# A decoder layer with two attentions: outputs stored as halves and summed in the finish, transposes six steps behind in half 0

## The chip, the cores and the metric

The kernel runs on one core of one Trainium2 chip. The metric is the device time of one execution in microseconds. The kernel before took 2151.33 us, the median of three runs (2150.57 to 2156.12).

## The reference

One decoder layer with two attentions side by side, on 2048 tokens plus 16 learned meta tokens in front, width 1024, float32. Everything comes out of one input projection of 6400 columns.

```python
xn = rms_norm(h, norm_gain[l])
proj = xn @ w_in[l]
sb_q, sb_k, sb_v, sw_q, sw_k, sw_v, sb_z, sw_z, g_sb, g_sw = jnp.split(proj, offsets, axis=-1)
o_sb = stick_breaking_attention(sb_q, sb_k, sb_v, valid)      # 8 heads of 64, all earlier keys
o_sw = sliding_window_sink_attention(q, k, sw_v, sinks, valid) # 16 query heads, 2 key heads, window 128
y_sb = (o_sb * jax.nn.silu(sb_z)) @ w_branch_sb[l]
y_sw = (o_sw * jax.nn.silu(sw_z)) @ w_branch_swa[l]
merged = jax.nn.sigmoid(g_sb) * y_sb + jax.nn.sigmoid(g_sw) * y_sw
h = h + merged @ w_out[l]
return rms_norm(h, final_norm_gain)[:, BLOCK:]
```

The first attention weighs keys by running products of sigmoids (a cumulative sum of logs in the reference), the second is a softmax over the block and the one before it, with a sink. What matters for this change is the line after each of them: the output o of an attention is multiplied by a gate and goes into a branch projection.

## The kernel before, in words

**Precision and tiling.** Most matmul operands are split into a high and a low part of type float32r, and a product is three matmuls (high times high, high times low, low times high). The sequence is processed backwards in four groups of 512 tokens. Groups 2 and 3 are half 0, groups 0 and 1 half 1.

**Stages.** For each half: projections with banded (sliding-window) attention woven in, then gate columns with stick-breaking attention woven in, then more gate columns. Half 0 ends its gates in a "fast" stage with seven products for eight. After both halves comes the finish: for half 0 and then half 1, the branch projections, the merge, the output projection, and the final norm.

**Order.** TensorE's instructions stand in the order of the program, which a function `weave` mixes from a main stream (projections) and a side stream (an attention) by estimated costs. The other engines and the DMA queue are ordered by the framework's planner, by its own estimate of time; each then works strictly in that order. All DMAs are issued by one queue, SP's (`DMA`, line 58).

**Banded attention** (`window`, `values`). For one block of 128 queries and four heads, matmuls accumulate 128 rows in the only PSUM bank `ps_o`: rows 0 to 63 come from the high part of v, rows 64 to 127 from the low part, and the output is their sum. ACT copies the low 64 rows to SBUF (line 757), and two DVE additions (line 761) put the sum into a tile `os`, of which there is one. After four blocks `os` is stored to DRAM as `ow`, in two DMAs.

**Stick-breaking attention** (`stick`). A step is one block of 128 queries against up to 512 keys. `row`: two matmuls into `ps_z` (line 861), a sigmoid on ACT (line 865), and a running product by DVE (`tensor_tensor_scan`, lines 873 and 875). `turn`, LT = 5 steps later: up to four transposes by TensorE into one of two banks `ps_t` (line 886), which ACT and DVE then evict as a high and a low part (`evac_split`, lines 114 and 115). `values`, two steps after that: matmuls into `ps_o` (line 912). At the end of a head and group ACT copies `ps_o` (line 917), a DMA brings its low 64 rows to partitions 0 to 63, POOL adds the two (line 919), and a DMA stores the sum as `od`. In half 0 a head has 12 steps, in all 96; in half 1 it has 28. DVE applies the causal mask in half 0, POOL in half 1.

**Gated tiles** (`gated`). For the branch projections each output tile of 128 x 512 is loaded with its gate (`ow` with `zw`, `od` with `zs`), multiplied by DVE (line 199), cast to the high part by ACT (line 201), and the low part is the difference by DVE (line 202). There are 48 such tiles: 16 of `ow` for half 0, made beside the last gates of half 1 with staging buffers `tmp` (nine of them, shared with the gates); 16 of `ow` for half 1, made while half 0's output projection runs, eight for each group, with staging buffers `a` (AB = 6, shared with other small tiles); and 16 of `od`, eight in each half's finish, with staging buffers `a`.

**Finish** (`finish`). Per half the banded branch comes first: projections `d` = 0, 1, 2 for the first group, the same three for the second group, then `d` = 3 to 7 for both groups. One projection is 24 matmuls (lines 225 to 227) and is multiplied by its gate on DVE (line 253). The `od` tiles are emitted when `d` = 4 begins. Then come the stick-breaking branch, the merge, and the output projection (lines 282 to 284).

Of the kernel before, what the change touches and what calls it, by code (L numbers as in the profile page):

```python
# [7 lines left out]
F32 = mybir.dt.float32  # L8
# [3 lines left out]
ALU = mybir.AluOpType  # L12
# [4 lines left out]
P = 128  # L17
# [4 lines left out]
GT = 512  # L22
RW = GT + NM
NB = SEQ // P
EPS = 1e-6
LT = 5
XS = 4
QB = 4
MID = 3
# [18 lines left out]
def tile_kernel(ctx, tc, x, xt, meta, metat, gain, w_in, w_sb, w_sw, w_out, sinks, fgain,  # L48
# [8 lines left out]
    def DMA(dst, src):  # L57
        nc.sync.dma_start(*(t.bitcast(F32) if t.dtype == F32R else t for t in (dst, src)))
# [28 lines left out]
    def dram(name, shape, dt=F32):  # L87
        return dp.tile(shape, dt, tag=name, name=name)
# [5 lines left out]
    zw = [[dram(f"zw{p}_{g}", [P, GT]) for g in range(4)] for p in range(8)]  # L94
    gs = [[dram(f"gs{p}_{g}", [P, GT]) for g in range(4)] for p in range(8)]
    gw = [[dram(f"gw{p}_{g}", [P, GT]) for g in range(4)] for p in range(8)]
    od = [[dram(f"od{p}_{g}", [P, GT]) for g in range(4)] for p in range(4)]
    ow = [[dram(f"ow{p}_{g}", [P, GT]) for g in range(4)] for p in range(8)]
    ksv = dram("ksv", [P, 4, P], F32R)
    msd = [dram(f"msd{p}", [NM, P]) for p in range(2)]  # L100
    vsv = dram("vsv", [P, 2 * P], F32R)
# [91 lines left out]

    def gated(src, zz, k, g, ring, stg):

        a, b = stg(), stg()
        DMA(a, src[k][g])
        DMA(b, zz[k][g])
        V.tensor_tensor(a, a, b, op=ALU.mult)
        h, l = ring(), ring()  # L200
        A.copy(h, a)
        V.tensor_tensor(l, a, f32(h), op=ALU.subtract)
        return h, l

    def finish(ringl, osw, first):
# [23 lines left out]
        for half, groups in enumerate(halves):  # L229
# [10 lines left out]
            ws_of = {}  # L240
            order = [(d, g) for ds in ([0, 1, 2], *([d] for d in range(3, 8))) for g in groups for d in ds]
            for d, g in order:
                if d == 4 and g == groups[0]:
                    osb = {(k, g): gated(od, zs, k, g, ringr, lambda: small("a", AB)) for g in groups for k in range(4)}
                if d not in ws_of:
                    ws_of[d] = first if half == d == 0 else weights(d * P, w_sw)
                ws = ws_of[d]
                acc = bank()
                project(acc, ws, [osw[k, g] for k in range(8)])
                gt = small("gt", 3)  # L250
                DMA(gt, gw[d][g])
                part[d, g] = ringr(F32)
                V.tensor_tensor(part[d, g], acc, gt, op=ALU.mult)
# [82 lines left out]
    def tmp(dt=F32, rows=P):  # L336
        return tp.tile([rows, GT], dt, tag="tmp", name="tmp", bufs=9)
# [259 lines left out]
    def window(half, groups, sp):  # L597
# [145 lines left out]
        def values(s, g, i, st):  # L743
            kv = s // 2
            blk = 4 * (g - groups[0]) + i
            if i == 0:
                os_[0] = sp.tile([P, 2, GT], F32, tag="os", name="os", bufs=1)
            o = ps("o")
            ph, pl, pm = st["p"]
            oc = o.rearrange("p (a q) -> p a q", a=4)  # L750
            for n in range(2):
                c = slice(HB * n, HB * n + HB)
                v = vv[:, blk + n, kv, :]
                for j, (lv, rp) in enumerate(((v, ph), (v, pl), (dv[kv, blk][:, n, :], pm))):
                    T.matmul(oc[:, :, c], lhsT=lv, rhs=rp[:, :, c], start=j == 0, stop=j == 2)  # L755
            t = tmp(rows=64)
            A.copy(t, o[64:128])
            ov = o[0:64].rearrange("p (b a q) -> p b a q", b=2, a=2)
            tv = t.rearrange("p (b a q) -> p b a q", b=2, a=2)
            for a in range(2):  # L760
                V.tensor_tensor(os_[0][64 * a:64 * a + 64, :, i * P:(i + 1) * P],
                                ov[:, :, a, :], tv[:, :, a, :], op=ALU.add)
            if i == 3:
                for pr in range(2):
                    DMA(ow[2 * s + pr][g], os_[0][:, pr, :])

        os_ = [None]
        ending = []
# [24 lines left out]
    def stick(groups, bp, sums_of={}):  # L793
        kt, vc = {}, {}
        rows_of = {}
        for g in groups:
            w = wm[g % 2]
            G.memset(f32(w), 1.0)
            G.affine_select(out=w, in_=f32(w), pattern=[[-1, 4], [0, P]], compare_op=ALU.is_equal, fill=0.0,
                            base=-64 - 4 * g, channel_multiplier=1)  # L800
# [101 lines left out]
        def values():  # L902

            h, g, v, wh, wl, first, last = av_todo.pop(0)
            st = state[h, g]
            if first:
                st["o"] = ps("o")
            o = st["o"]
            n = wh.shape[1]
            for r in (wh, wl):  # L910
                if r is not None:
                    T.matmul(o[:, :n], lhsT=v, rhs=r, start=first and r is wh, stop=last)  # L912
            if last:
                p, a = divmod(h, 2)
                t = tmp(rows=64)
                u = tmp()
                A.copy(u, o)  # L917
                DMA(t, u[64:128])
                G.tensor_tensor(t, u[0:64], t, op=ALU.add)  # L919
                DMA(od[p][g][64 * a:64 * a + 64], t)  # L920
            return 0.22 if wl is None else 0.43

        steps = [(h, g, n, j) for h in range(8) for g in reversed(groups) for n in range(4 - g) for j in range(4)]
        n = len(steps)
        turned = []
        for s in range(n + LT + 3):
            if s < n:
                row(*steps[s])
                yield 0.45 if s >= LT else 1.31
            t = s - LT  # L930
            if 0 <= t < n:
                turn(*steps[t])
                turned.append(s)
                yield 0.43
                if sum(steps[t][1:3]) == steps[t][3] == 3:
                    turn_meta(*steps[t][:2])
                    turned.append(s)
                    yield 0.43
            while av_todo and turned[0] < s - 1:
                del turned[0]  # L940
                yield values()
# [296 lines left out]
    for half, groups in enumerate(halves):  # L1238
# [57 lines left out]
        with tc.tile_pool(name=f"sb{half}", bufs=1, side="left") as bp:  # L1296
            hsplit[0], vsplit[0] = True, False
            next_sums = {g: sums() for g in halves[1]} if half == 0 else {}
            side = stick(groups, bp, next_sums)
            drain(tiles_by_tile(gts[few:few + 1], groups))  # L1300
            rest = 28 - FAST - PLAIN if half == 0 else 23
            cost_sb = 8 * sum(4 * (4 - g) for g in groups) * 1.31 + 16 * 0.75 + LT * 0.86
            ratio = cost_sb / ((rest - few - 1) * 10.4)
            weave(tiles_by_tile(gts[few + 1:rest], groups), side, ratio)
            if half == 0:
                hsplit[0] = vsplit[0] = True
                plain = [mk() for mk in gts[rest:rest + 2]]
            drain(side)
            if half == 0:
                t, u = (bp.tile([P, GT], F32, tag="wh", name="sum", bufs=3)[:, :8] for _ in range(2))  # L1310
                for n, ssq in enumerate(next_sums.values()):
                    V.tensor_tensor(t[:, 4 * n:4 * n + 4], ssq[:, 0], ssq[:, 1], op=ALU.add)
                rs = tp.tile([P, 8], F32, tag="rs8", name="rs", bufs=1)
                rsqrt(rs, t, tp, t=u)
                rs0, rs1 = rs[:, :4], rs[:, 4:]
# [90 lines left out]
```

## Time and profile before

| | |
|---|---|
| median of three runs | 2151.33 us |
| the profiled execution, its own time | 2154.71 us |
| its span, first to last instruction | 2153.0 us |
| TensorE matmuls, busy | 2118.0 us (98%) |
| VectorE (DVE), busy | 1460.8 us (68%) |
| ScalarE (ACT), busy | 1074.4 us (50%) |
| GpSimd (POOL), busy | 353.2 us (16%) |
| DMA, mean | 180 GB/s |
| mean granted TensorE clock | 0.998 |

How to read it: TensorE is busy nearly all the time, and what is left is idle time spread over the stages. "PE" rows are matmuls, "PEld" rows are weight loads, which run beside them. A row such as "PE ps_t L886 <- DVE wtl L115: 5.8, 11, 1.1" says that matmuls of line 886 waited 5.8 us in total, 11 times, at most 1.1 us, and that a DVE instruction of line 115 ended the wait. In a row of a timeline, the bracket at the end gives the idle time of the engine before it and what ended it. Times of single rows are microseconds from the start of the span.

### The profile page before, as it was taken

The page shows a single profiled execution, that of the slowest core. Times are in us where ns is not written, and L with a number is a line of the kernel's source. Part 1 is how long each engine was busy: PE and PEld are TensorE (multiplying, and loading weights), DVE is VectorE, ACT ScalarE, POOL GpSimd, SP SyncE. Part 2 cuts the span into 40 slices and gives each one's busy share as a digit, 9 for nine tenths or more (in the row PEclk, how much of TensorE's full clock was granted, in tenths as well). Part 3 has the DMA queues.
Part 4 walks back from the last instruction along what each step waited for, and adds up shares of the span by engine and source line. Part 5 has one row for each costly group of instructions (what it writes and reads, how often), then busy time and mean ns, then how long its engine had stood idle before and what let it go on. Part 6 is the DMA issues. An engine that isn't in the chain of part 4 may idle for free.

```text
span 2153.0 us, 30793 instructions
## 1 busy us (share of the span) xinstructions
PE 2118.0 (98%) x10658; PEld 1752.7 (81%) x10658; DVE 1460.8 (68%) x2319; ACT 1074.4 (50%) x2461; POOL 353.2 (16%) x526
## 2 busy tenths in 40 slices
PE   8999999999999999999999999999999999999998
PEld 6788888777778888888888888888888888787886
DVE  7788876877787563777747888878774436453453
ACT  6577775555554334777744555555553213221121
POOL 2234453121110000233310000000100121000000
PEclk9999999999999999999999999999999999999999
DMA  9755454766547674444345333343424976467422
GB/s 331 277 190 194 174 192 165 254 196 193 168 139 252 225 238 158 153 159 162 134 163 173 123 128 118 118 126 96 122 86 157 358 255 219 163 219 272 149 97 88
DMA packets 167740, 386.74 MB, mean 180 GB/s; under 512 B 24192, under 2 KB 28032, under 8 KB 167584
## 3 DMA queue, kind: packets, MB, share of 16 engines
q1 hardware_dynamic: 167584, 384.78, 52.8%
q8 instruction: 84, 1.38, 0.3%
q14 instruction: 72, 0.59, 0.1%
HBM read 237.35 MB, written 140.98 MB: 176 GB/s over the span
## 4 chain that ended last, share of the span: by engine, by line
PE 80%; DVE 7%; ACT 5%; DMA 4%; issue 2%; POOL 1%; SPq 1%; ACTq 0%; POOLq 0%; DVEq 0%
PE ps_g L406 10%; PE ps_g L407 10%; PE ps_g L408 10%; PE ps_o L912 6%; PE ps_z L861 5%; PE ps_t L886 5%; PE ps_z L699 2%; PE ps_o L755 2%; PE ps_g L226 1%; DMA xq<-in_x 1%; PE ps_g L227 1%; PE ps_g L225 1%; PE ps_z L226 1%; PE ps_z L227 1%; PE ps_z L225 1%
## 5 line engine op out<-in xcount | busy, mean ns | idle before, releaser
L406 PE MATMUL ps_g<-xh,wh 128*128 128x512 f32 x1296 | 532.8, 411 | 8.8 <-ACT xh L1090 6.9
L408 PE MATMUL ps_g<-xh,wl 128*128 128x512 f32 x1296 | 509.5, 393 | 0.0
L407 PE MATMUL ps_g<-xl,wh 128*128 128x512 f32 x1296 | 509.2, 393 | 0.0
L875 DVE TENSOR_TENSOR_SCAN row<-row 128x512 f32<-128x512 f32 (+4 forms) x256 | 308.4, 1205 | 84.2 <-POOL row L870 36.6
L408 PEld LDWEIGHTS ps_g<-xh,wl 128*128 128x128 f32 x1296 | 243.8, 188 | 54.5 <-DVE wl L111 0.2
L406 PEld LDWEIGHTS ps_g<-xh,wh 128*128 128x128 f32 x1296 | 245.0, 189 | 48.3 <-ACT xh L1090 6.9
L407 PEld LDWEIGHTS ps_g<-xl,wh 128*128 128x128 f32 x1296 | 245.0, 189 | 38.0 <-DVE xl L1091 1.3
L865 ACT ACTIVATE row<-ps_z 128x512 f32<-128x512 f32 (+1 forms) x320 | 172.2, 538 | 194.2 <-PE ps_z L861 163.1
L114 ACT ACTIVATE wth<-ps_t 128x512 fp32r<-128x512 f32 (+1 forms) x320 | 170.5, 533 | 70.7 <-PE ps_t L886 68.4
L115 DVE SCALAR_TENSOR_TENSOR wtl<-ps_t,wth 128x512 fp32r<-128x512 f32 (+1 forms) x320 | 188.1, 588 | 20.2 <-ACT wth L114 19.7
L861 PE MATMUL ps_z<-kt,q 128*128 128x512 f32 (+3 forms) x640 | 185.8, 370 | 0.2 <-DMA q<-qd 0.2
L886 PE MATMUL ps_t<-ident,row 128*128 128x128 f32 x1088 | 172.4, 274 | 5.9 <-DVE wtl L115 5.8
L886 PEld LDWEIGHTS ps_t<-ident,row 128*128 128x128 f32 x1088 | 134.6, 140 | 43.5 <-DVE wtl L115 10.9
L861 PEld LDWEIGHTS ps_z<-kt,q 128*128 128x128 f32 x640 | 117.8, 188 | 24.3 <-DMA q<-qd 0.6
L912 PE MATMUL ps_o<-wth,vc 128*128 128x512 f32 (+1 forms) x320 | 130.1, 407 | 0.6 <-ACT tmp L917 0.6
L912 PE MATMUL ps_o<-wtl,vc 128*128 128x512 f32 (+1 forms) x320 | 116.7, 365 | 0.0
L707 ACT ACTIVATE sc<-sc,nm 128x129 f32<-128x129 f32 x256 | 100.0, 393 | 31.4 <-DVE nm L705 30.2
L919 POOL TENSOR_TENSOR tmp<-tmp 64x512 f32<-64x512 f32 x32 | 45.5, 1422 | 341.9 <-DMA tmp<-tmp 181.2
L111 POOL TENSOR_TENSOR wl<-raw,wh 128x1024 fp32r<-128x1024 f32 (+1 forms) x28 | 61.4, 2191 | 194.0 <-ACT wh L108 176.9
L108 ACT CAST wh<-raw 128x1024 fp32r<-128x1024 f32 (+1 forms) x44 | 42.7, 971 | 99.6 <-PE ps_g L226 29.7
L873 DVE TENSOR_TENSOR_SCAN row<-row,mask 128x512 f32<-128x512 f32 (+2 forms) x64 | 72.2, 1134 | 29.3 <-ACT row L865 21.1
L561 ACT ACTIVATE tmp<-ps_g 128x512 f32<-128x512 f32 x84 | 50.2, 597 | 59.7 <-PE ps_g L408 53.3
(434 smaller groups left out, 4130.3 us busy)
## 6 DMA issues: line engine op xcount, KB each, us to landing
wh<-h_in_w_in SPq DMA_DIRECT2D x66, 512.0 KB, 3.4
wl<-l_in_w_in SPq DMA_DIRECT2D x66, 512.0 KB, 5.0
raw<-in_w_in SPq DMA_DIRECT2D x50, 512.0 KB, 5.3
h_in_w_in<-wh SPq DMA_DIRECT2D x50, 512.0 KB, 2.7
l_in_w_in<-wl SPq DMA_DIRECT2D x50, 512.0 KB, 3.8
q<-qd SPq DMA_DIRECT2D x128, 128.0 KB, 3.2
vc<-vd SPq DMA_DIRECT2D x48, 256.0 KB, 2.8
kd<-tmp SPq DMA_DIRECT2D x32, 256.0 KB, 3.8
```

The source lines that it names most:

```text
L114: A.activation(h, acc, AF.Copy, scale=scale)
L115: V.scalar_tensor_tensor(l, acc, scale, f32(h), op0=ALU.mult, op1=ALU.subtract)
L406: T.matmul(acc, lhsT=wh[:, k, :], rhs=xh[g][:, k, :], start=k == 0, stop=False)
L407: T.matmul(acc, lhsT=wh[:, k, :], rhs=xl[g][:, k, :], start=False, stop=False)
L408: T.matmul(acc, lhsT=wl[:, k, :], rhs=xh[g][:, k, :], start=False, stop=k == KT - 1)
L707: A.activation(sc[:, hh, :], sc[:, hh, :], AF.Exp, bias=nm[:, hh:hh + 1], accum_out=den[:, hh:hh + 1])
L861: T.matmul(z[:, :w], lhsT=lq, rhs=kt[h][:, k0:k0 + w], start=t == 0, stop=t == 1)
L865: A.activation(r[:, :w], z[:, :w], AF.Sigmoid, scale=-1.0)
L873: V.tensor_tensor_scan(r[:, :w], r[:, :w], mask[:, :w], 1.0, op0=ALU.mult, op1=ALU.max)
L875: V.tensor_tensor_scan(r[:, :w], r[:, :w], r[:, :w], last[j] if n else 1.0, op0=ALU.mult, op1=ALU.min)
L886: T.transpose(tr[:, j * P:(j + 1) * P], rows_of[h, g, n - (j > i), j][:, k0:k0 + P], ident)
L912: T.matmul(o[:, :n], lhsT=v, rhs=r, start=first and r is wh, stop=last)
```

## The change

Four edits that belong together:

- The banded attention copies the whole bank of 128 rows with one ACT copy; the DVE additions are gone. The tile `os` now holds two blocks, and after every second block four DMAs of 128 KB store the high and low halves to `ow`, which is twice as large.
- The stick-breaking attention stores the two halves of its output to `od`, also doubled, straight from ACT's copy; the DMA between partitions and POOL's addition are gone.
- `gated` loads both halves and adds them on DVE before it multiplies by the gate: one more staging buffer, one more DMA of 256 KB and one more DVE addition for each of the 48 tiles. The `od` tiles in the finish are emitted when `d` = 3 begins.
- LT, the lag from `row` to `turn`, is six steps in half 0 and stays five in half 1.

```diff
-LT = 5
+LT = (6, 5)
...
-    od = [[dram(f"od{p}_{g}", [P, GT]) for g in range(4)] for p in range(4)]
-    ow = [[dram(f"ow{p}_{g}", [P, GT]) for g in range(4)] for p in range(8)]
+    od = [[dram(f"od{p}_{g}", [2, P, GT]) for g in range(4)] for p in range(4)]
+    ow = [[dram(f"ow{p}_{g}", [2, P, GT]) for g in range(4)] for p in range(8)]
...
     def gated(src, zz, k, g, ring, stg):
 
-        a, b = stg(), stg()
-        DMA(a, src[k][g])
+        a, b, c = stg(), stg(), stg()
+        DMA(a, src[k][g][0])
+        DMA(c, src[k][g][1])
         DMA(b, zz[k][g])
+        V.tensor_tensor(a, a, c, op=ALU.add)
         V.tensor_tensor(a, a, b, op=ALU.mult)
...
-                if d == 4 and g == groups[0]:
+                if d == 3 and g == groups[0]:
                     osb = {(k, g): gated(od, zs, k, g, ringr, lambda: small("a", AB)) for g in groups for k in range(4)}
...
-            if i == 0:
-                os_[0] = sp.tile([P, 2, GT], F32, tag="os", name="os", bufs=1)
+            if i % 2 == 0:
+                os_[0] = sp.tile([P, 4, 2 * P], F32, tag="os", name="os", bufs=1)
...
-            t = tmp(rows=64)
-            A.copy(t, o[64:128])
-            ov = o[0:64].rearrange("p (b a q) -> p b a q", b=2, a=2)
-            tv = t.rearrange("p (b a q) -> p b a q", b=2, a=2)
-            for a in range(2):
-                V.tensor_tensor(os_[0][64 * a:64 * a + 64, :, i * P:(i + 1) * P],
-                                ov[:, :, a, :], tv[:, :, a, :], op=ALU.add)
-            if i == 3:
+            A.copy(os_[0][:, :, i % 2 * P:(i % 2 + 1) * P], oc)
+            if i % 2:
                 for pr in range(2):
-                    DMA(ow[2 * s + pr][g], os_[0][:, pr, :])
+                    for n in range(2):
+                        DMA(ow[2 * s + pr][g][n][:, (i - 1) * P:(i + 1) * P].rearrange("(a d) t -> d a t", a=2),
+                            os_[0][64 * n:64 * n + 64, 2 * pr:2 * pr + 2, :])
...
+        lt = LT[groups[0] == 0]
...
-                t = tmp(rows=64)
                 u = tmp()
                 A.copy(u, o)
-                DMA(t, u[64:128])
-                G.tensor_tensor(t, u[0:64], t, op=ALU.add)
-                DMA(od[p][g][64 * a:64 * a + 64], t)
+                for n in range(2):
+                    DMA(od[p][g][n][64 * a:64 * a + 64], u[64 * n:64 * n + 64])
...
-        for s in range(n + LT + 3):
+        for s in range(n + lt + 3):
             if s < n:
                 row(*steps[s])
-                yield 0.45 if s >= LT else 1.31
-            t = s - LT
+                yield 0.45 if s >= lt else 1.31
+            t = s - lt
...
-            cost_sb = 8 * sum(4 * (4 - g) for g in groups) * 1.31 + 16 * 0.75 + LT * 0.86
+            cost_sb = 8 * sum(4 * (4 - g) for g in groups) * 1.31 + 16 * 0.75 + LT[half] * 0.86
```

## The prediction

> **What bounds the kernel now.** I read the page first, then a table of stages, then what TensorE waited for. The page gives the frame:
>
> ```profile
> span 2153.0 us, 30793 instructions
> PE 2118.0 (98%) x10658; PEld 1752.7 (81%) x10658; DVE 1460.8 (68%) x2319; ACT 1074.4 (50%) x2461; POOL 353.2 (16%) x526
> ```
>
> TensorE (PE) is the bound, and the change gives it no matmul and takes none away. So its time can move only in the 35 us in which PE sits idle, and in new idle time. The table of stages shows where that is; its columns are length, then busy time (and count) of PE, PEld, DVE, ACT and POOL, the granted clock, the DMA share and GB/s:
>
> ```profile
> 75.00:375.00 300.00, 294.42 (x1655) 249.78 (x1654) 234.32 (x461) 207.68 (x594) 124.96 (x203) 1.00 0.53 187
> 375.00:613.00 238.00, 229.90 (x1259) 189.44 (x1258) 185.67 (x245) 134.33 (x303) 44.91 (x27) 1.00 0.62 194
> 860.00:1125.00 265.00, 261.44 (x1427) 224.06 (x1426) 189.46 (x388) 188.32 (x535) 86.76 (x170) 1.00 0.45 154
> 1125.00:1641.00 516.00, 515.95 (x2780) 430.61 (x2779) 408.16 (x483) 275.47 (x535) 40.30 (x79) 1.00 0.38 119
> 1641.00:1697.00 56.00, 56.00 (x249) 46.36 (x248) 21.66 (x31) 17.94 (x29) 6.07 (x3) 1.00 0.86 305
> 1921.00:2011.00 90.00, 89.78 (x384) 71.80 (x384) 33.63 (x56) 11.06 (x20) 0.00 (x0) 1.00 0.71 248
> ```
>
> The rows are, in order: the banded attention of half 0 (idle 5.6 us), the stick-breaking attention of half 0 (idle 8.1), the banded attention of half 1 (3.6), the stick-breaking attention of half 1 (0.05), the last gates with the first gated tiles (0), and the start of half 1's finish (0.22). There is something to win in the first three, nothing in the fourth, and something to lose in the last two. The list of waits names the releasers:
>
> ```profile
> PE ps_t L886 <- DVE wtl L115: 5.8, 11, 1.1
> PE ps_o L755 <- DVE os L761: 2.5, 3, 1.6
> PE ps_z L699 <- DVE sc L703: 1.0, 4, 0.4
> PE ps_g L226 <- DVE ringl L202: 0.2, 1, 0.2
> ```
>
> All four wait for DVE. The first three are in the attentions, where the change relieves DVE. The fourth is in the finish, where the change loads it.
>
> **Banded attention (values).** Today each block has one ACT copy of 64 rows and two DVE additions that read and then free the one bank ps_o. Now one ACT copy of 128 rows frees it.
>
> ```profile
> L761 DVE TENSOR_TENSOR os<-ps_o,tmp x128: 386/417/419, 136.0 to 1119.0; 64x256 f32<-64x256 f32 x128
> L757 ACT COPY tmp<-ps_o x64: 564/584/590, 134.6 to 1117.9; 64x512 f32<-64x512 f32 x64
> L865 ACT ACTIVATE row<-ps_z 128x512 f32<-128x512 f32 (+1 forms) x320 | 172.2, 538 | 194.2 <-PE ps_z L861 163.1
> ```
>
> DVE loses 128 x 0.417 = 53 us. ACT's copy keeps its 512 columns; a 128-row read of PSUM with 512 columns takes 0.54 us (L865), as much as L757's 0.58, so ACT pays nothing. The three waits on os go: -2.5. The waits on sc (1.0) lose half, since they too wait for DVE: -0.5, bounds 0 and -1. New is a wait of the ACT copy for the stores of the single os tile, now every second block, with four stores in place of two every fourth:
>
> ```profile
> 191.25 0.79 SPq L58 DMA_DIRECT2D ow<-os  x2
> 221.05 0.80 SPq L58 DMA_DIRECT2D ow<-os  x2
> ow<-os SPq DMA_DIRECT2D x32, 256.0 KB, 2.2
> ```
>
> Four blocks take 221.05 - 191.25 = 29.8 us, one 7.5. Four stores issue in 1.6 us and land 2.2 later, 3.8 after the copy, so 3.7 us are left and I take nothing. If SP's queue is held (96 more issues stand ahead of weight loads), ACT waits, and behind it the exponentials and PSUM copies on which PE waits: up to +4, about one microsecond in a quarter of the 16 pairs of a half.
>
> **Stick-breaking attention (row sums and lag).** Gone are 32 SBUF-to-SBUF copies and 32 POOL additions; od's one store becomes two that wait for ACT alone, so the number of DMAs stays. POOL's time itself is free, but not what it does to DVE:
>
> ```profile
> L875 DVE TENSOR_TENSOR_SCAN row<-row 128x512 f32<-128x512 f32 (+4 forms) x256 | 308.4, 1205 | 84.2 <-POOL row L870 36.6
> 510.49 1.27 POOL L919 TENSOR_TENSOR tmp<-tmp 64x512 f32<-64x512 f32 x1 [15.37 <-ACT row L865]
> 511.73 2.38 POOL L111 TENSOR_TENSOR wl<-raw,wh 128x1024 fp32r<-128x1024 f32 x1
> 510.58 4.64 DVE L875 TENSOR_TENSOR_SCAN row<-row 128x528 f32<-128x528 f32 x1 [0.40 <-ACT row L867]
> 516.05 0.55 PE L886 MATMUL ps_t<-ident,row 128*128 128x128 f32 x3 [1.10 <-DVE wtl L115]
> 518.43 0.44 PE L886 MATMUL ps_t<-ident,row 128*128 128x128 f32 x2 [0.50 <-DVE wtl L115]
> ```
>
> A scan that takes 1.2 us on average took 4.64: longer by 3.4, nearly what the two POOL operations ran (1.27 + 2.38). The eviction L115 stood behind it, and PE then waited 1.10 and 0.50 us for a bank. Without L919 the scan keeps only L111's share, some 1.2 us earlier, which covers most of that. From half 0's 5.8 us I take -2.5: this event's 1.6 and 0.9 of the other 4.2. Bounds 0 and -5.8. In half 1 the same contention exists, but PE idles 0.05 us: nothing. SP's queue no longer waits for L919 ahead of the q and xq loads; I count that in the 2.5.
>
> The lag of six in half 0 I price at zero. It gives the scans one more step before their transposes, but PE's waits here are for the evictions of the two ps_t banks (L115), and these come as soon after their transposes as before. It shifts which evictions meet which scans, which can go either way; the bound is one step, 238 us over 104 steps = 2.3 us, to both sides. The ratio of the weave changes by 0.86 in 142, which only shifts gate columns.
>
> **Finish: 48 gated tiles, each with one more load of 256 KB and one more DVE addition.** The tight place is the start of half 1's finish, where eight tiles of group 1 are made while PE runs three projections of group 0:
>
> ```profile
> 1925.92 0.69 DVE L199 TENSOR_TENSOR a<-a 128x512 f32<-128x512 f32 x1
> 1933.28 0.68 DVE L199 TENSOR_TENSOR a<-a 128x512 f32<-128x512 f32 x1
> 1934.70 0.69 DVE L202 TENSOR_TENSOR ringl<-a,ringl 128x512 fp32r<-128x512 f32 x1 [0.74 <-ACT ringl L201]
> 1935.31 0.68 DVE L199 TENSOR_TENSOR a<-a 128x512 f32<-128x512 f32 x1
> a<-od SPq DMA_DIRECT2D x16, 256.0 KB, 5.5
> a<-ow SPq DMA_DIRECT2D x16, 256.0 KB, 3.8
> a<-zw SPq DMA_DIRECT2D x16, 256.0 KB, 4.0
> 1921.28 0.39 PE L225 MATMUL ps_g<-ringl,wh 128*128 128x512 f32 x1
> 1938.07 0.40 PE L225 MATMUL ps_g<-ringl,wh 128*128 128x512 f32 x1
> 1943.02 0.50 PE L225 MATMUL ps_g<-ringl,wh 128*128 128x512 f32 x1
> 1943.75 0.50 PE L226 MATMUL ps_g<-ringl,wh 128*128 128x512 f32 x1 [0.22 <-DVE ringl L202]
> ```
>
> Today one tile costs DVE 0.68 (product), 0.74 (waiting for ACT's cast) and 0.69 (difference), a period of 2.03 us; six buffers "a" hold three tiles in flight. The eighth tile arrives 0.5 us late: the matmul of 1943.75 could have followed at 1943.25. With three buffers a tile only two are in flight. A buffer pair then turns in load 4.0 + issue 0.32 + DVE 0.69 + 0.69 + 0.74 + 0.69 = 7.1 us for two tiles, 3.6 each. The first tile ends at 1925.9 + 2.8 = 1928.7, the second at 1931.5, the eighth at 1931.5 + 3 x 7.1 = 1952.8. PE wants it at 1943.25, so it stands 9.5 us, 9.0 more than now. The lower bound is a DVE that puts the next addition into the 0.74 us gap with all loads in time: 8 x 2.1 + three evictions L253 of 0.68 = 18.9, done at 1944.8, +1.1. The upper takes the landing of a<-od, 5.5: a turn of 8.6, done at 1957.3, +13.6. I take 9, as the loads of today's rows already come into a DMA share of 0.71 over that stage.
>
> Idle PE also costs clock:
>
> ```profile
> 634.00:637.00 3.00, 3.00 (x15) 2.45 (x15) 2.88 (x5) 0.02 (x1) 0.00 (x0) 1.00 0.29 70
> 637.00:641.00 4.00, 2.33 (x9) 1.30 (x8) 3.11 (x5) 4.00 (x7) 0.00 (x0) 0.95 0.61 242
> 641.00:644.00 3.00, 3.00 (x9) 2.32 (x8) 3.00 (x7) 2.62 (x5) 0.00 (x0) 0.50 0.95 265
> ```
>
> After 1.7 idle us in four, the granted clock was 0.50 for the next three, where 9 matmuls ran in place of 15. Waits of 9.5 us within 12 should bring one or two such stretches of 3 us at half speed: +2, bounds 0 and 3.4. The Trainium skill ("TensorE: Matmul & The Clock Gate", Part 1) has the clock fall after at least one idle window of about 3.4 us. By that rule waits cut up by the arrival of single tiles would cost no clock (rival 4); the rows above show a fall after 1.7 us of idling, so the trace does not agree, and it decides.
>
> In half 0's finish 16 such tiles run through nine "tmp" buffers beside the gates: 16 x 256 KB = 4.2 MB more, at 305 GB/s / 0.86 = 355 GB/s another 11.8 us of transfers.
>
> ```profile
> L199 DVE TENSOR_TENSOR tmp<-tmp x16: 684/692/2056, 1659.4 to 1695.8; 128x512 f32<-128x512 f32 x16
> ```
>
> The last is ready at 1695.8 + 2.1 = 1697.9. PE starts this finish at 1697 and, as in half 1, comes to the second group 16.8 us later (1938.07 - 1921.28), at 1713.8. The cover is 15.9 us, 4.1 more than needed. If weight loads stand behind these in SP's queue and get the whole delay, 11.8 - 4.1 = 7.7. I take +2. The eight od tiles, emitted one projection earlier, have 24 loads instead of 16 on SP; they are due only at 2011 and I give them nothing, with one turn (3.6) as upper bound.
>
> **Sum.** -2.5 - 0.5 - 2.5 + 9 + 2 + 2 = +7.5 us. The profiled execution took 2154.71, which makes 2162.2; it lies 3.4 above the median, and against the median of 2151.33 the forecast is 2159.
>
> **Rivals.** (1) Faster: SP and DVE overlap the new additions in the cast's gap, and gated tiles come every 2.1 us, as the lower bound has it. It decides from a period below about 2.4 us in half 1: then 1.1 replaces 9 and 2, half 0 costs nothing, and -5.5 + 1.1 = -4.4 remains; with all of the 5.8 us of bank waits gone in place of 2.5 it is -7.7, and -10 if the lag also gives its 2.3. Its middle is -7.7, 2144, within 2141 to 2147. For it speaks DVE's share in that stage (33.6 of 90 us), against it the six buffers. (2) The two sides cancel: half 1 costs half as much (a turn of 5 to 6 us), 4.5 + 1, total 0, 2150 to 2157; the DMAs' medians hold both fast and slow landings. (3) Half 0's finish stalls too: +7.7 in place of 2, 2165, and up to 2170 with the upper bound in half 1. For it speaks the DMA share of 0.86, against it the 15.9 us of cover. (4) The clock holds through the chopped waits: 2 less, 2157; against it stands the row with 0.50. (5) The lag doesn't do what its name says: that is in the forecast, at zero; if it did, the forecast would read 2157.
>
> **How the numbers follow.** A measurement here tells differences over 0.3%, 6.5 us, so "same" is 2144.9 to 2157.8. Chances: forecast 0.33 (2154 to 2164; 0.26 of it above 2157.8), rival 1 0.24 (0.19 of it faster), rival 2 0.20 (same), rival 3 0.18 (slower), rival 4 0.05 (same). Slower: 0.26 + 0.18 = 0.44. Faster: 0.19. Same: 0.07 + 0.05 + 0.20 + 0.05 = 0.37. The range 2144 to 2168 leaves out the faster half of rival 1 and the top of rival 3; the forecast's own is 2154 to 2164.
>
> **What would show it.** In the list of waits, PE ps_g L226 <- DVE ringl L202 should grow from 0.2 to about 9 us near 1940, with a period of the group-1 tiles near 3.6 us and a row of clock 0.50 behind it; PE ps_o L755 <- DVE os should be gone; PE ps_t L886 should fall from 5.8 to about 3; scans over 2 us beside POOL should be rarer. A period near 2 us there, or PE waits on "a" loads elsewhere, makes the forecast wrong.

## The result, and the profile after

The changed kernel takes **2172.05 us** (median of 6 runs, 2169.81 to 2174.27), the kernel before 2154.68 us beside it (6 runs, 2150.57 to 2157.32): a ratio of **1.0082**, 95% interval 1.007 to 1.0094. The forecast was 2159 in a range of 2144 to 2168: slower was right, the amount was not. The profiled execution took 2170.74.

The page after, first lines:

```profile
span 2168.9 us, 30858 instructions
PE 2124.4 (98%) x10658; PEld 1757.3 (81%) x10658; DVE 1438.9 (66%) x2239; ACT 1066.7 (49%) x2461; POOL 303.2 (14%) x494
```

The same matmuls, 22 us less of DVE and 50 us less of POOL, and a span longer by 15.9 us. The table of stages of the changed kernel shows where (columns as in the prediction):

```profile
75.00:375.00 300.00, 294.97 (x1661) 250.66 (x1661) 217.26 (x403) 202.27 (x593) 126.44 (x202) 1.00 0.63 205
375.00:613.00 238.00, 232.96 (x1272) 194.13 (x1272) 178.14 (x250) 139.58 (x309) 19.66 (x12) 0.99 0.60 192
860.00:1125.00 265.00, 262.62 (x1428) 225.33 (x1427) 160.25 (x313) 178.94 (x524) 82.25 (x169) 1.00 0.54 172
1641.00:1697.00 56.00, 47.91 (x199) 38.46 (x197) 28.73 (x39) 14.94 (x23) 6.27 (x3) 0.94 0.96 350
1921.00:2011.00 90.00, 84.97 (x338) 65.47 (x337) 45.18 (x79) 12.18 (x24) 0.00 (x0) 0.92 0.80 281
```

The attentions (first three rows) idle less than before: 5.0, 5.0 and 2.4 us against 5.6, 8.1 and 3.6. The fourth row, 1641 to 1697, full before (249 matmuls), now idles 8.1 us and has 199 matmuls at a clock of 0.94; the fifth, 1921 to 2011, idles 5.0 us at 0.92. The waits of PE, over the whole span, by releaser:

```profile
PE ps_g L408 <- ACT xh L1087: 6.9, 1, 6.9
PE ps_g L408 <- ACT tmp L563: 6.0, 2, 4.6
PE ps_g L227 <- ACT tmp L563: 5.2, 1, 5.2
PE ps_z L860 <- ACT row L864: 3.2, 2, 2.7
PE ps_g L227 <- ACT ringl L203: 2.9, 3, 1.5
PE ps_g L228 <- DVE ringl L204: 2.0, 3, 0.9
PE ps_t L885 <- DVE wtl L115: 1.6, 3, 1.1
```

Line numbers have moved: the sum in `gated` is L200, its product L201, the cast L203, the difference L204; the projections are L227 to 229, and L563 is the sigmoid in `gate`, which copies a gate column out of PSUM. The first row stands in the kernel before too, with the same 6.9 us. The wait for `os` is not in the list any more, and the wait for L115 fell from 5.8 to 1.6; 3.2 us of waits for L864, a sigmoid of the stick-breaking attention on ACT, are new beside it. The waits for L203 and L204 (4.9) are the forecast one, in half 1. The second and third rows, 11.2 us, are new and were not forecast: PE waits for a **gate's** eviction, not for a gated tile.

The stages of several kernels can be compared by matmuls that mark them: the last row of half 1's stick stage, the first projection of each half's finish, and the first matmul of half 1's output projection. In the kernel before these start at 1629.6, 1696.6, 1921.3 and 2056.3 us. The table gives, from one profiled execution of each, by how many microseconds the stretch up to each is longer (+) or shorter than in the kernel before. What comes after the fourth is the same everywhere.

| kernel | to the end of half 1's stick stage | last gates with the first 16 tiles | half 0's finish | half 1's finish to its output projection | span |
|---|---|---|---|---|---|
| the change | -10.9 | +14.3 | +1.6 | +10.9 | 2168.9 |
| e1 stick part alone | -5.0 | 0 | +0.4 | +0.9 | 2149.3 |
| e2 banded part alone | 0 | +7.4 | +1.6 | +10.7 | 2172.8 |
| e3 change, lag five | -5.4 | +10.6 | +1.0 | +9.8 | 2169.0 |
| e4 c in ring buffers | -8.9 | +31.9 | +6.2 | +4.3 | 2186.6 |
| e5 narrow c | -12.0 | +0.9 | +0.5 | +8.4 | 2150.8 |
| e6 own buffers for gates | -8.7 | 0 | +6.2 | +10.1 | 2160.6 |
| e7 e6 and c of group 1 apart | -6.3 | 0 | +3.1 | +4.7 | 2154.5 |
| e8 e1, banded summed by pairs | -5.6 | 0 | +0.8 | +0.2 | 2148.4 |

Five of these kernels do not differ in the first stretch (the change, e4 to e7), and give -6.3 to -12.0 there, -9.4 in the mean: single executions scatter by that much in that column. (The profiled execution was the fastest of its kernel's runs for e2 to e5 and e8, the slowest for e6.) The other columns repeat within about 1 us where the kernels agree, but for half 0's own stalls: the change, e2 and e3 share the edits that bear on the last gates, and lose 14.3, 7.4 and 10.6 us there.

### The profile page after: what moved, and what is told of

It reads as the page before. It is cut to its first block, busy times and chain, and to the rows that moved or that the text cites. A ratio compares the mean times of both kernels' runs of the same rounds, so it can differ in the third digit from the quotient of the medians.

```text
span 2168.9 us, 30858 instructions
## 1 busy us (share of the span) xinstructions
PE 2124.4 (98%) x10658; PEld 1757.3 (81%) x10658; DVE 1438.9 (66%) x2239; ACT 1066.7 (49%) x2461; POOL 303.2 (14%) x494
## 5 line engine op out<-in xcount | busy, mean ns | idle before, releaser
L874 DVE TENSOR_TENSOR_SCAN row<-row 128x512 f32<-128x512 f32 (+4 forms) x256 | 293.4, 1147 | 91.0 <-ACT row L864 40.2
L864 ACT ACTIVATE row<-ps_z 128x512 f32<-128x512 f32 (+1 forms) x320 | 172.0, 538 | 194.5 <-PE ps_z L860 174.7
L115 DVE SCALAR_TENSOR_TENSOR wtl<-ps_t,wth 128x512 fp32r<-128x512 f32 (+1 forms) x320 | 188.8, 590 | 26.5 <-ACT wth L114 25.9
L111 POOL TENSOR_TENSOR wl<-raw,wh 128x1024 fp32r<-128x1024 f32 (+1 forms) x28 | 60.9, 2176 | 349.6 <-ACT wh L108 233.5
L108 ACT CAST wh<-raw 128x1024 fp32r<-128x1024 f32 (+1 forms) x44 | 42.7, 971 | 106.8 <-DMA a<-zs 19.0
L872 DVE TENSOR_TENSOR_SCAN row<-row,mask 128x512 f32<-128x512 f32 (+2 forms) x64 | 67.7, 1063 | 29.2 <-ACT row L866 15.6
L869 POOL TENSOR_SCALAR_AFFINE_SELECT row<-row 128x128 f32<-128x128 f32 x64 | 20.2, 315 | 468.8 <-ACT row L864 442.3
L563 ACT ACTIVATE tmp<-ps_g 128x512 f32<-128x512 f32 x84 | 50.1, 597 | 57.3 <-PE ps_g L410 43.7
```

The source lines that it names most:

```text
L115: V.scalar_tensor_tensor(l, acc, scale, f32(h), op0=ALU.mult, op1=ALU.subtract)
L864: A.activation(r[:, :w], z[:, :w], AF.Sigmoid, scale=-1.0)
L872: V.tensor_tensor_scan(r[:, :w], r[:, :w], mask[:, :w], 1.0, op0=ALU.mult, op1=ALU.max)
L874: V.tensor_tensor_scan(r[:, :w], r[:, :w], r[:, :w], last[j] if n else 1.0, op0=ALU.mult, op1=ALU.min)
```

## How half 0 came to wait

The timeline of the changed kernel around the end of the gates, the rows on the path (start, duration, engine, line; the idle time before it in the bracket):

```profile
1677.69 2.34 POOL L111 TENSOR_TENSOR wl<-raw,wh 128x1024 fp32r<-128x1024 f32 x1 [9.85 <-DMA tmp<-zw]
1678.52 2.06 DVE L200 TENSOR_TENSOR tmp<-tmp 128x512 f32<-128x512 f32 x1 [1.94 <-DMA tmp<-ow]
1680.66 0.60 ACT L563 ACTIVATE tmp<-ps_g 128x512 f32<-128x512 f32 x1 [3.05 <-DMA tmp<-ow]
1681.31 0.79 PE L408 MATMUL ps_g<-xh,wh 128*128 128x512 f32 x1 [4.55 <-ACT tmp L563]
...
1694.48 0.39 PE L410 MATMUL ps_g<-xh,wl 128*128 128x512 f32 x1
1694.68 1.04 ACT L108 CAST wh<-raw 128x1024 fp32r<-128x1024 f32 x1 [8.77 <-PE ps_g L409]
1695.63 0.61 ACT L203 CAST ringl<-tmp 128x512 fp32r<-128x512 f32 x1
1695.80 2.34 POOL L111 TENSOR_TENSOR wl<-raw,wh 128x1024 fp32r<-128x1024 f32 x1 [15.77 <-ACT wh L108]
1696.27 2.41 DVE L204 TENSOR_TENSOR ringl<-tmp,ringl 128x512 fp32r<-128x512 f32 x1 [6.10 <-ACT ringl L203]
1698.61 0.68 DVE L200 TENSOR_TENSOR tmp<-tmp 128x512 f32<-128x512 f32 x1
1699.37 0.60 ACT L563 ACTIVATE tmp<-ps_g 128x512 f32<-128x512 f32 x1 [3.13 <-issue]
1700.02 0.80 PE L227 MATMUL ps_g<-ringl,wh 128*128 128x512 f32 x1 [5.15 <-ACT tmp L563]
```

A sigmoid L563 writes a `tmp` tile, one of nine, taken in turn. With three buffers for each gated tile in place of two, the buffer whose turn it is still belongs to a gated tile. First case: the sum L200 that frees it waits 1.94 us for a load of `ow`; the sigmoid starts 0.08 us after the sum's end, PE 0.05 after the sigmoid, having stood for 4.55. (The brackets of the two sigmoids name the load and "issue"; that it was the sum is read from the times: both sigmoids start 0.08 us after a sum L200 ended.)

Second case: ACT stood 8.77 us at L108, the cast of the next weights, whose buffer PE frees only when it ends the gate column. Behind L108 on ACT waited the cast L203 of a gated tile, behind that on DVE the difference L204 and the sum L200, and behind that the sigmoid which empties the bank that PE needs. So the path runs from PE's last matmul (1694.48) back to PE (1700.02) through two ACT, two DVE and one more ACT instruction, 5.15 us with PE idle. This second case varies most: in e2 and e3 the wait at the same place was 1.4 us. The sum of the first case (2.06) and the difference of the second (2.41) took three times the usual 0.69 and more, and both lie beside POOL's L111. The Trainium skill ("SBUF — State Buffer", "Who interferes with whom") has a DVE operation with two inputs in SBUF contend with a POOL operation that reads SBUF, over a port pair that only one of them holds at a time; the two pairs of rows agree, at a cost of 1.4 and 1.7 us.

## The experiments

**e1 and e2: the halves of the change.** e1 keeps the stick-breaking part (halves of `od`, lag of six, tiles emitted at `d` = 3), e2 the banded part (halves of `ow`), lag five. `gated` loads and adds the second half only where the source has one:

```diff
-        a, b, c = stg(), stg(), stg()
+        a, b = stg(), stg()
+        if src is od:      # e2: ow
+            c = stg()
...
```

> Only od is kept as halves (with the lag of six in half 0 and the od tiles emitted at d = 3); the banded attention and its ow tiles are as before. Theory (the loss comes from the third staging buffer and the extra load of the ow tiles): neither the 14.3 us ahead of half 0's finish nor the 10.9 us in half 1's finish appear, the gain of the first stick-breaking stage (4.7 us) stays, the gain of the banded stages (3.2 and 1.5 us) goes: about 5 us less than before, ratio 0.998. Rival (the finish loses because of the od tiles and their move to d = 3): a loss of 10 us or more stays, ratio 1.003 or above.

> Only ow is kept as halves; the stick-breaking attention, its od tiles, the lag of five and d = 4 are as before. Theory: both losses stay whole (14 and 11 us), the banded gains of some 4.7 us stay, the stick-breaking gain goes: about 20 us more than before, ratio 1.009. Rival (od tiles cause the loss): faster than before by about 5 us.

e1: **2148.5 us** (9 runs), ratio 0.9973 (0.9964 to 0.9983), a little faster than the kernel before. e2: 2176.87, ratio 1.0102 (1.0086 to 1.0117). All of the loss belongs to the halves of `ow`; the 16 `od` tiles with their third buffer cost nothing that can be seen (+0.4 and +0.9 in e1's finishes). The banded gain that was expected to stay in e2 is not in its first column (0): half 0's stick stage begins 5.4 us earlier than before (first row at 380.0 in place of 385.4), but its rows then take 6.3 us longer (222.7 in place of 216.4), with 8.6 us of waits for L115. Why they do is open.

**e3: the change with a lag of five** (`LT = (5, 5)`).

> The changed kernel with a lag of five in both halves. If the lag is worth nothing, as the prediction had it, the first stick-breaking stage keeps its gain of 4.7 us within 1 us and the time is that of the changed kernel within 3 us. Rival (the lag makes the gain): that stage loses 3 to 5 us and the time rises by as much.

2172.24 us, ratio 1.0078 (1.0063 to 1.0093): within the intervals of the change itself. The two profiles differ by 5.5 us in the first column and by 3.7 the other way in the second; both are within the scatter.

**e4: c, the second half, in ring buffers** for half 0's 16 tiles and for group 1's eight, so that the staging buffers hold as many tiles as before.

```diff
-        a, b, c = stg(), stg(), stg()
+        a, b, c = stg(), stg(), (more or stg)()
...
+                    osw[k, g] = gated(ow, zw, k, g, ringl, tmp, lambda: ringl(F32))
```

> The changed kernel, but the second half of an ow tile is staged in a free tile of a ring of 32 instead of a third tmp or a buffer (for half 0's 16 tiles and the eight of group 1). Bytes, DMAs and additions are those of the changed kernel. If the number of staging buffers is what stalls TensorE: the 14.3 us ahead of half 0's finish fall below 4, the 10.9 us in half 1 below 4, and the time is about 2152, ratio 0.999. If the bytes are what stalls it (DMA share 0.96 in the stage before the finish): the 14.3 us stay above 9 and the 10.9 above 6.

2192.45 us, ratio 1.0178 (1.0161 to 1.0195). Half 1's loss fell from 10.9 to 4.3. Half 0's rose to 31.9, where the theory had it fall below 4, and by the number the rival (bytes) had come true. For half 0 it was no clean test, though: the loads of c went out one tile at a time. Rows of e4's DMA queue:

```profile
1679.63 0.42 SPq L58 DMA_DIRECT2D ringl<-ow  x1
...
1684.84 0.42 SPq L58 DMA_DIRECT2D ringl<-ow  x1
...
1690.09 0.43 SPq L58 DMA_DIRECT2D ringl<-ow  x1
...
1695.38 0.54 SPq L58 DMA_DIRECT2D ringl<-ow  x1
```

One tile in 5.3 us; why the loads went out so is open. The waits in the same stretch of e4 are the change's own in a larger form. Three of its sigmoids, at 1672.31, 1696.39 and 1719.06, start 0.04 us after a difference L204 ended, and the profile names that difference as what released them: the later a gated tile frees its `tmp` buffer, the longer PE stands for a sigmoid.

```profile
PE ps_g L409 <- ACT tmp L564: 16.8, 2, 10.0
PE ps_g L227 <- ACT tmp L564: 8.7, 1, 8.7
```

**e5: c is 16 columns wide**, with all its buffers, DMAs and instructions. It leaves the other 496 columns of the second half out of the sum.

```diff
-        DMA(c, src[k][g][1])
+        DMA(c[:, :16], src[k][g][1][:, :16])
...
-        V.tensor_tensor(a, a, c, op=ALU.add)
+        V.tensor_tensor(a[:, :16], a[:, :16], c[:, :16], op=ALU.add)
```

> The changed kernel, but of the second half only 16 of 512 columns are loaded and added (the rest of the second half is left out of the sum). Staging buffers, DMA count and order stay, the bytes (0.25 MB a tile) and most of the addition go. If the buffers alone stall TensorE: the step ahead of half 0's finish stays above 8 us and that in half 1's finish above 7 us, time about 2166 or more. If the bytes (slow landings at a DMA share of 0.96) are needed for the stall: both steps fall below 4 us, time about 2150.

2155.4 us, ratio 1.0009 (1.0 to 1.0018). It takes away two things at once, the bytes and most of the addition's time (0.17 us in place of 0.69), and with them half 0's loss (+0.9) but not half 1's (+8.4). The waits of e5 from 1600 us on:

```profile
PE ps_g L228 <- DVE ringl L204: 3.3, 2, 1.7
PE ps_g L227 <- ACT ringl L203: 1.3, 2, 0.7
PE ps_g L227 <- ACT tmp L563: 0.7, 1, 0.7
```

So half 0's loss needs the bytes or the long addition, and e5 does not say which; half 1 stalls without either, from the third buffer and the load that comes with it.

**e6: the last five gate columns write their sigmoid into another pool's buffers**, idle at that time.

```diff
+    own = [False]
...
-            e = tmp()
+            e = (ring_x if own[0] else tmp)()
```

> The changed kernel, but the last five gate columns of half 1 take their sigmoid's tile from the idle ring xs of four instead of tmp, so they never compete with the gated tiles for a buffer. Theory (TensorE stands because the sigmoid that empties ps_g waits for a tmp buffer held by gated tiles): the step ahead of half 0's finish falls from 14.3 to below 4 us, half 1's 10.9 stay, time about 2160. Rival (the sigmoid is late because it stands behind casts in ACT's order, or because of the bytes): the step stays above 9 us, time 2168 or more.

2160.81 us, ratio 1.0032 (1.0019 to 1.0045). The last gates take as long as before (0 in the table), with every load and addition of the change in place. The waits of e6 from 1600 us on have no row for a sigmoid:

```profile
PE ps_g L227 <- ACT ringl L203: 3.4, 3, 1.7
PE ps_g L227 <- DVE ringr L255: 3.1, 1, 3.1
PE ps_g L228 <- DVE ringl L204: 1.9, 4, 0.8
```

This is the direct test of half 0: the tiles were not late for the projections, they were in the gates' way. Two things follow from the edit beside the gates' own buffers: the nine `tmp` now serve the gated tiles alone, and the planner orders ACT anew (at 1678.02 a sigmoid stands directly behind the weight cast L108, no longer behind a cast L203). Part of the gain is lost again in half 0's finish, as a wait of 3.1 for a gate product L255, which stands on DVE behind the `od` tiles. Of the rest of that +6.2, about 1 is waits in the output projection, and most of what is left fits the clock, 0.54 from 1760 to 1763, just behind the wait.

**e7: e6, and c of group 1 in ring buffers** as in e4.

> As the run before, and in addition the second half of the eight tiles of group 1 is staged in free tiles of the ring ringr, so that three tiles are again in flight on the six buffers a. Theory: half 1's step falls from 10.9 to about 4.3 (as in the run with rings), the step ahead of half 0's finish stays below 4, time about 2153 or less, at or below the kernel before. Rival: if bytes decide, half 1's step stays above 9.

2155.96 us, ratio 1.0006 (0.9996 to 1.0015): 16 us of the change's 17 are gone, at the same number of loads and additions, though the time stays above the 2153 that was expected. Half 1 keeps 4.7.

**e8: e1 with the banded attention's whole-bank copy, but summed on the spot**: for every pair of blocks a DMA between partitions and one DVE addition, `ow` stored once as before.

```diff
+                    DMA(tv, os_[0][64:128, 2 * pr:2 * pr + 2, :])
+                    V.tensor_tensor(tv, os_[0][0:64, 2 * pr:2 * pr + 2, :], tv, op=ALU.add)
```

> od as halves with the lag of six, as in the run that changes the stick-breaking side alone; the banded attention copies its whole bank with one ACT copy as in the changed kernel, but the halves are brought together right there, by a DMA between partitions and one DVE addition for each pair of blocks, so ow and its gated tiles stay as before. If the banded gain comes from freeing ps_o early: the two banded stages keep 3 and 1.5 us, nothing is lost in the finish, and the time is 4 to 5 us below the run with od alone (2148.5), ratio 0.995. Rival (the gain comes from the additions that DVE no longer makes): the gain is 1 us or less, or it turns into waits for the moved halves; 2148 to 2152.

2153.17 us, ratio 0.9998 (0.9988 to 1.0008), slower than theory and rival had it: its profiled execution was as short as e1's, its runs were not. In that execution half 0's stick stage begins at 386.3 us, no earlier than before (385.4), while it begins at 380.0 to 382.9 in the profiles without any sum by DVE in the banded stage. So freeing `ps_o` by one copy did not bring the banded gain by itself.

**e9 to e12: what the stick part's gain is made of.** e9 is the kernel before with a lag of six, e10 is e1 with a lag of five, e11 e1 with seven, and e12 is e1 once more.

> The kernel before with one edit: a lag of six steps from row to turn in half 0. Theory: the lag itself is worth 4 to 6 us, because the transposes of a step then no longer come to TensorE's order before the scan and the evictions of the step ahead are done; the first stick-breaking stage shortens by about 5 us as in the kernel with the stick-breaking edits alone (-4.85), POOL's addition L919 or not, and the time falls to about 2149. Rival: the lag is worth nothing (as the prediction had it) and the gain of that kernel comes from the dropped copies between partitions and additions of POOL; then the time stays at 2154 within 1.5 us and the stage within 2 us of before.

> The stick-breaking edits alone (halves of od, added in the finish), but with the lag left at five. Theory (the lag makes the gain): the first stick-breaking stage loses its gain of 4.85 us and is as long as before or up to 3 us longer, and the time is 2153 to 2157. Rival (the dropped copies and POOL additions make the gain): 2148 to 2150, with a stage 3 to 5 us shorter than before.

> The stick-breaking edits alone with a lag of seven in half 0. Theory (the lag gives the scans and evictions time): most of TensorE's waits for L115 in that stage were gone at six (some 8 us idle before, 3 to 4 us left), so a seventh step gains 0 to 2 us more, 2146.5 to 2149. Rival: twelve row buffers with a lag of seven leave ACT waiting for a buffer, and the time rises to 2151 or more.

> The kernel with the stick-breaking edits alone (lag of six, halves of od), as in the first set of runs, timed a second time beside new runs of the kernel before. If its gain there (ratio 0.9973) is a real effect of the two edits together, the ratio lies at 0.9965 to 0.998 again, a time of 2147 to 2150. Rival: the lag alone gave 0.9999, lag five with halves 0.9988 and lag seven 0.9994; if the edits are worth 1 to 3 us and the first timing was on the lucky side, the ratio is 0.9985 to 0.9995, a time of 2150 to 2153.

e9: 2153.12 us (11 runs), ratio 0.9999 (0.999 to 1.0008). e10: 2151.05 (11), 0.9988 (0.9979 to 0.9997). e11: 2151.83 (11), 0.9994 (0.9985 to 1.0003). e12: **2148.17** (6), 0.9967 (0.9954 to 0.998). The gain of halves and lag together is real, 6 to 7 us in two sets of runs, and by the medians it is more than the two alone, 0 and 2. That surplus is not secured: the intervals of e10 and e1 overlap, and the sets were timed apart. e10 lies between its theory (2153 to 2157) and its rival (2148 to 2150), and for e11 the rival came (2151 or more).

The profiles don't settle why. PE's waits for L115 in the first stick stage, 375 to 613 us, were 5.8 us (11 times) before; in e9, e12 and e10, in this order:

```profile
PE ps_t L887 <- DVE wtl L115: 4.4, 4, 2.7
```

```profile
PE ps_t L894 <- DVE wtl L115: 4.0, 3, 2.6
```

```profile
PE ps_t L894 <- DVE wtl L115: 2.4, 5, 0.7
```

All three have fewer such waits than before, and in microseconds the lag of five with halves (e10) has the least. From its first row to its last the stage is about 5 us shorter in the profiles of e9 and e12 alike, and 3.5 in e10's; but e9's profiled execution was the fastest of its eleven (2149.5, median 2153.12), so it does not speak for the others. A lag of seven trades these waits for 3.6 us on ACT's sigmoids. The theory that the lag alone makes the gain fell with e9; that the dropped copies alone make all of it is made unlikely by e10. How the two act together stays open.

## Why the prediction was wrong

Against the profiled execution of before (2154.71) the sum was +7.5; the profiled execution after stands 16.0 above it. Step by step:

**Banded and stick-breaking attention: -5.5 forecast, -10.9 measured** up to the end of half 1's stick stage. The direction was right: the wait for `os` is gone, L115's fell to 1.6, where "about 3" was expected, and scans over 2 us in the two stick stages fell from 14 to 2. The size was low, by 1 to 6.5 us in the five profiles that share this part, 4 in their mean. In the changed kernel's profile 4.7 us are won before half 0's stick stage begins (first row at 380.7 in place of 385.4), 4.6 in its rows (211.8 in place of 216.4), and 1.4 from there to the first row of half 1's. So the banded stages brought up to 6, about twice the 3.0 forecast. For half 0's stick stage the prediction took 2.5 of 5.8 us of bank waits; 4.2 of them went, but 3.2 of waits for ACT's sigmoids came in their place. All waits of PE in that stage are 8.2 before and 4.8 after: 3.4 gone. How much of it is the lag is open (e9's rows, with the lag alone, take 211.6).

**The lag at zero** stands, taken alone (e9: 0.9999) and in the whole change (e3). With halves of `od` it looks worth 3 to 4 us (e1 and e12 against e10), which would be beyond its bound of 2.3, but the intervals do not secure that.

**Half 1's finish: 9 + 2 forecast, 10.9 measured.** The sum is right, and so is the cause: e5 shows 8.4 without the bytes and the long addition, e4 and e7 that giving the third buffer elsewhere takes off some 6. DVE in the changed kernel, from the first sum of group 1 to the last difference, and the matmul that takes up the eighth tile:

```profile
1930.90 0.68 DVE L200 TENSOR_TENSOR a<-a 128x512 f32<-128x512 f32 x1
...
1956.31 0.69 DVE L204 TENSOR_TENSOR ringl<-a,ringl 128x512 fp32r<-128x512 f32 x1
1957.05 0.80 PE L228 MATMUL ps_g<-ringl,wh 128*128 128x512 f32 x1 [0.94 <-DVE ringl L204]
```

That is 26.1 us for eight tiles, where the prediction's turns made 26.9 (1925.9 to 1952.8); before it was 17.8. PE takes up the eighth tile 30.8 us after this finish began (at 1926.27), where it was 22.5 before (1943.75 - 1921.28): 8.3 later, against 9.0 forecast. The 2.6 that remain of 10.9 are the clock's, against 2 forecast. The list of waits shows only 4.9 of the 8.3, not the "about 9" that was expected, because PE ran slow in between, in time in which it would have waited for the tile anyway. The stretches behind the waits:

```profile
1945.00:1949.00 4.00, 2.26 (x8) 0.98 (x6) 2.66 (x5) 0.62 (x1) 0.00 (x0) 1.00 0.93 317
1949.00:1953.00 4.00, 2.27 (x4) 1.08 (x4) 2.50 (x5) 1.23 (x2) 0.00 (x0) 0.53 0.78 258
1953.00:1957.00 4.00, 2.49 (x4) 0.79 (x3) 2.84 (x5) 0.62 (x1) 0.00 (x0) 0.50 0.85 273
1957.00:1961.00 4.00, 3.95 (x9) 3.15 (x10) 2.58 (x4) 0.91 (x2) 0.00 (x0) 0.50 0.87 263
1961.00:1963.00 2.00, 2.00 (x6) 1.56 (x5) 0.69 (x1) 0.33 (x1) 0.00 (x0) 0.54 0.96 340
1963.00:1967.00 4.00, 4.00 (x18) 3.19 (x17) 0.68 (x2) 0.00 (x0) 0.00 (x0) 1.00 0.86 326
```

From 1949 to 1963 the clock is half, some 14 us in place of the "one or two stretches of 3". At full speed 18 matmuls take 4 us, 0.22 each; at 0.50 without idling 9 take 4, 0.44 each. Only the 13 slow matmuls from the eighth tile on cost time, 13 x 0.22 = 2.9. So the price of +2 came out nearly right with a stretch at half speed that is more than twice as long as forecast: that is luck. By the Trainium skill's rule of a whole idle window ("TensorE: Matmul & The Clock Gate", Part 1), waits chopped into pieces of at most 1.5 us, tile by tile, would have cost no clock (rival 4): these rows decide against it, as the ones of before did.

**Half 0's finish: +2 forecast, 14.3 + 1.6 measured. This is the step that failed.** (The 14.3 is the dearest of three profiles, as the table shows; the least is 7.4.) The prediction asked one thing of these 16 tiles, whether they would be ready when the projections want them: "The cover is 15.9 us, 4.1 more than needed." It named the resource that the tiles share, nine "tmp" buffers beside the gates, and then priced only their transfers. What it left out is the other user of these buffers: a sigmoid that empties a PSUM bank takes its place in the same turn, so a tile that is early for its own consumer holds up the gates, for which there is no cover at all. Of the 14.3, the waits make 11.2, 3.1 of them through the two DVE operations beside L111; the clock makes most of the rest, at half speed from about 1679.5 to 1686. The 1.6 behind it fit the clock too, 0.51 from 1700 to 1703. e6 shows the buffers as the cause, e5 that with short loads and additions they would have been enough.

**The rivals.** Rival 3, half 0's finish stalls too, at 2165 to 2170, was the nearest: +13.7 to +18.7 over the 2151.33 it was counted from, and +17.4 measured. Its mechanism, weight loads delayed in SP's queue, was not the one: PE waits for sigmoids, not for weights. Rival 1, gated tiles every 2.1 us, fell with 26.1 us for eight, 3.3 each. Rival 2's half price in half 1 fell with 10.9; its total of 0 also leaves out half 0's 2. Of the things to be shown, the one that was announced as making the forecast wrong, waits of PE elsewhere in the finish, came, though not on loads of "a".

The median of three runs from which the forecast was counted, 2151.33, was low: in later sets the kernel before had medians of 2153.3 to 2155.3. That explains 3.4 us of the 13 by which the forecast missed; half 0 less the larger gain of the attentions (13.9 - 5.4) makes 8.5, and the median after lies 1.3 above its profiled execution.

## What to carry to other kernels

When a step takes one more buffer from a pool, list everyone who takes from that pool in turn, and ask of each what waits behind it: the cost is set by the user with the least slack (here a sigmoid that frees a PSUM bank), not by the step that was changed. Moving an addition from a stage where it is hidden to the one that ends last can cost more than it saves: the same kind of edit gains for `od` (e1, 0.997, with the lag), whose tiles are due long after they are made, and loses for `ow` (e2, 1.010). A cheap pair of trials is to narrow a transfer while keeping its buffers (e5), and to give the buffers' other user its own while keeping the transfers (e6). Here either took half 0's loss away, and half 1's yielded mainly to other buffers for c (e4, e7).

## What the runs showed of the hardware

In these traces short waits cost TensorE's clock soon and for long. In half 0 PE's last matmul before the wait began at 1676.37, and the clock fell before the next one at 1681.31 (the table of stages, cut fine):

```profile
1674.00:1676.00 2.00, 2.00 (x11) 1.65 (x10) 0.80 (x2) 0.62 (x1) 0.00 (x0) 1.00 0.95 362
1676.00:1680.00 4.00, 0.76 (x4) 0.30 (x2) 2.06 (x2) 1.04 (x1) 2.31 (x1) 0.94 1.05 391
1680.00:1683.00 3.00, 1.69 (x4) 1.40 (x5) 2.88 (x5) 1.71 (x3) 0.03 (x1) 0.50 1.04 402
1683.00:1686.00 3.00, 3.00 (x8) 2.32 (x8) 2.23 (x5) 1.24 (x2) 0.00 (x0) 0.50 1.03 378
1686.00:1689.00 3.00, 3.00 (x13) 2.43 (x13) 1.33 (x2) 0.00 (x0) 0.00 (x0) 0.94 0.95 294
```

A mean of 0.94 over four microseconds is half speed for the last 0.5 of them: it fell at about 1679.5, some 2.7 us after the end of the matmul (1676.8), and it came back at about 1686.4, 5 us after PE had work again. A single wait of 1.4 us (up to 1665.58) did not lower it: the clock is 1.00 from 1660 to 1674. In the list of waits none of this shows: by it alone half 1's stall would have looked half as dear as it was.
